# Add and gelu of two flat arrays on one core: rows of 63.5, 64 and 0.5 KB in three blocks instead of rows of 128 KB

## The chip, the core and the metric

The kernel runs on one core of a Trainium2 chip. The core has a tensor engine (PE, not used here), a vector engine (DVE, VectorE), a scalar engine with activation functions (ACT, ScalarE), a general engine (POOL, GpSimd) and a queue engine (SP, SyncE) that here issues the transfers between DRAM (HBM) and the on-chip memory SBUF. The transfers are carried out by 16 DMA engines. SBUF has 128 partitions; a tile here is 128 rows, one a partition. The metric is the device time of one execution in microseconds.

## The reference

Two float32 arrays of 1024 x 4096 are added, and the tanh form of gelu is taken of the sum, element by element:

```python
z = x + y
return (0.5 * z * (1 + np.tanh(np.sqrt(2 / np.pi) * (z + 0.044715 * z ** 3)))).astype(np.float32)
```

Each array is 16.78 MB. Two are read and one is written: 50.33 MB. As every element stands by itself, an array may be cut into rows in any way, as long as x, y and the output are cut alike.

## The kernel before

Each array is seen as 128 rows of 32768 elements (TOT, 128 KB), one a partition (line 88). SBUF holds one tile z of 128 x 32768 for x, the sum and the result, and one tile y of 128 x 16384 (HALF), half a row, that y's two halves use one after the other. A small tile `one` serves to load the activation table early.

There are six transfers, two loads of x, two of y and two stores, each of 128 rows of 64 KB (lines 91 to 93: the halves of the rows). All are issued on SP's queue in a fixed order: y's first half, x's first half, x's second half, y's second half, the first store, the second store. `begin_early` moves the first two ahead of the barrier at the program's start. The second y load overwrites the y tile, so it waits for the adds of the first half. Each store waits for the gelus of its half. `wait_late` lets the program's end clean up while the last store runs, and makes only ACT wait for that store's landing.

The compute goes by 20 chunks of columns (line 94: two of 1024, seven of 2048, 512, 1536, six of 2048, 1024, 512, 512). Chunks 0 to 8 are the first half and 9 to 19 the second. An add (z + y into z) runs on DVE, for chunks 7, 8 and 12 on POOL. For some chunks (`copies`) ACT first copies z to PSUM, a second on-chip memory, and DVE's add reads one operand from there. ACT then takes the gelu of each chunk in place (`on_scalar` is ACT's order). `held` makes POOL's first add wait for DVE's add of chunk 1. A chunk waits for the loads that its columns lie in, by the overlap of column ranges (`over`, `needs`).

The order on each engine is written out by hand: four lists (`sp`, `pool`, `acts`, `dve`), issued as soon as what `needs` names has been issued. The waits on the chip follow from the tiles.

Of the kernel before, what the change touches and what calls it, by code (L numbers as in the profile page):

```python
# [66 lines left out]
def kernel(  # L67
# [12 lines left out]
    nc = tc.nc  # L80
    P = nc.NUM_PARTITIONS
# [3 lines left out]
    N, D = x.shape  # L85
    assert N % P == 0
    TOT = N // P * D
    xv, yv, ov = (a.rearrange("(p n) d -> p (n d)", p=P) for a in (x, y, out))

    HALF = TOT // 2  # L90
    xloads = [HALF, HALF]
    yloads = [16384, 16384]
    stores = [16384, 16384]
    chunks = [1024, 1024] + [2048] * 7 + [512, 1536] + [2048] * 6 + [1024, 512, 512]
    copies = {2: 0, 3: 2048, 4: 0, 5: 2048, 6: 0, 9: 0, 10: 512, 11: 2048}
    on_vector = [0, 1, 2, 3, 4, 5, 6, 9, 10, 11, 13, 14, 15, 16, 17, 18, 19]
# [4 lines left out]
    def ranges(sizes):  # L101
        ends = [sum(sizes[: i + 1]) for i in range(len(sizes))]
        assert ends[-1] == TOT
        return [(e - f, e) for e, f in zip(ends, sizes)]

    xr, yr, sr, cr = (ranges(r) for r in (xloads, yloads, stores, chunks))
# [4 lines left out]
    def over(rs, lo, hi):  # L111
        return [i for i, (a, b) in enumerate(rs) if a < hi and b > lo]
# [6 lines left out]
    zt = pool_sb.tile([P, TOT], fp32, tag="z", name="z")  # L119
    yt = pool_y.tile([P, HALF], fp32, tag="y", name="y")  # L120
# [6 lines left out]

    def load_x(i):
        a, b = xr[i]
        nc.sync.dma_start(out=zt[:, a:b], in_=xv[:, a:b])  # L130

    def load_y(i):
        a, b = yr[i]
        o = a % HALF
        nc.sync.dma_start(out=yt[:, o : o + b - a], in_=yv[:, a:b])  # L135

    def store(i):
        a, b = sr[i]
        nc.sync.dma_start(out=ov[:, a:b], in_=zt[:, a:b])

    def copy(c):
        a, b = cr[c]
# [21 lines left out]
    def earlier_user(c):  # L164
        lo, hi = copies[c], copies[c] + chunks[c]
        before = [k for k in copies if k < c and copies[k] < hi and copies[k] + chunks[k] > lo]
        return [(add, k) for k in before]

    sp = [(load_y, i) for i in over(yr, 0, HALF)] + [(load_x, 0), (load_x, 1)]
    sp += [(load_y, i) for i in over(yr, HALF, TOT)]  # L170
    sp += [(store, i) for i in range(len(stores))]
    pool = [(add, c) for c in on_gpsimd]
    dve = [(add, c) for c in on_vector]
# [3 lines left out]
        load_x: lambda i: [],  # L177
        load_y: lambda i: [(add, c) for c in over(cr, yr[i][0] - HALF, yr[i][1] - HALF)],
        copy: lambda c: [(load_x, i) for i in over(xr, *cr[c])] + earlier_user(c),
        add: lambda c: [(load_x, i) for i in over(xr, *cr[c])]  # L180
        + [(load_y, i) for i in over(yr, *cr[c])]
        + [(copy, k) for k in copies if k == c]
        + [(add, k) for h, k in held.items() if h == c],
# [55 lines left out]
```

## Time and profile before

| | |
|---|---|
| time, median of 3 runs | 120.08 us (119.96 to 120.28) |
| span of the profiled execution | 118.68 us (118.7 on the page) |
| around the span, to the median | 1.40 us |
| moved | 50.33 MB in 864 packets, 424 GB/s over the span |
| busy: DMA engines, ACT, DVE, POOL | 98.5%, 37%, 25%, 12% |
| first y load | issued at 0.00, first packet at 1.01 us |
| x's first half has landed | 41.3 us |
| second y load | issued at 54.86, landed at 80.0 us |
| stores | issued at 77.16 and 97.64 us |

The profiled execution has no device time of its own beside its span, so the median stands for it. A page gives the span, each engine's busy time, the DMA packets with their sizes, and the chain of work that ended last. A packet is one row's piece that one DMA engine moves; the trace has the begin, duration and size of each. A transfer here also has one packet of 4 bytes on each DMA engine, which tells the semaphore of its end. L130, L135 and L139 are the lines that issue x's loads, y's loads and the stores; L150 is the add, L162 the gelu and L143 the copy.

### The profile page before, as it was taken

Reading aid. Unit: us, or ns where it says so; the run is one execution under the profiler, and the core shown is the slowest. Engines: PE = TensorE matmul, PEld = TensorE weight load, DVE = VectorE, ACT = ScalarE, POOL = GpSimd, SP = SyncE. Lnnn points to the kernel's source line nnn. Section 1 sums busy time; section 2 is a strip of 40 time slices with the busy share of each in tenths; the row PEclk is TensorE's granted clock in tenths of the full one; section 3 lists DMA queues with packets and bytes.
Section 4 is the critical chain, followed back from the end, with each engine's and each line's share of the span. In section 5 each row is a group of like instructions: output and inputs, shape, how many; then the busy total and the mean of one; then the engine's idle time right before and its main releaser. Section 6 shows DMA issues by size and latency. Waiting matters only on the chain.

```text
span 118.7 us, 112 instructions
## 1 busy us (share of the span) xinstructions
DVE 29.1 (25%) x18; ACT 44.1 (37%) x30; POOL 13.8 (12%) x7
## 2 busy tenths in 40 slices
DVE  0000000000000099994000000009999920000000
ACT  5000000000000096792059999903799980000000
POOL 0000000000000029980000000009500000000000
DMA  9889988998899888998899888998899888988891
GB/s 353 353 375 641 398 353 353 596 464 353 353 420 618 376 353 353 618 442 353 353 508 552 353 353 375 641 398 353 353 552 508 353 353 353 707 353 353 353 641 66
DMA packets 864, 50.33 MB, mean 424 GB/s; under 512 B 96, under 2 KB 96, under 8 KB 96
## 3 DMA queue, kind: packets, MB, share of 16 engines
q1 hardware_dynamic: 864, 50.33, 98.5%
HBM read 33.55 MB, written 16.78 MB: 424 GB/s over the span
## 4 chain that ended last, share of the span: by engine, by line
DMA 56%; DVE 14%; ACT 10%; DVEq 1%; ACTq 0%; SPq 0%; issue 0%
DMA z<-in_x_dram 34%; DMA y<-in_y_dram 21%; DVE z L150 14%; ACT z L162 10%; DVEq L206 1%; ACTq L206 0%; SPq L135 0%; DVEq L150 0%
## 5 line engine op out<-in xcount | busy, mean ns | idle before, releaser
L162 ACT ACTIVATE z<-z 128x2048 f32<-128x2048 f32 (+3 forms) x20 | 29.7, 1555 | 5.5 <-DVE z L150 5.5
L143 ACT COPY ps<-z 128x2048 f32<-128x2048 f32 (+2 forms) x8 | 13.0, 1654 | 46.8 <-DMA z<-in_x_dram 45.1
L150 DVE TENSOR_TENSOR z<-z,y 128x2048 f32<-128x2048 f32 (+2 forms) x9 | 13.6, 1574 | 40.0 <-DMA z<-in_x_dram 40.0
L150 DVE TENSOR_TENSOR z<-ps,y 128x2048 f32<-128x2048 f32 (+2 forms) x8 | 15.6, 2016 | 25.4 <-DMA y<-in_y_dram 25.4
L150 POOL TENSOR_TENSOR z<-z,y 128x2048 f32<-128x2048 f32 x3 | 13.5, 4529 | 70.7 <-DVE z L150 43.4
L191 ACT ACT_TABLE_LOAD x1 | 1.3, 1283 | 1.3 <-PEq L223 1.3
L190 DVE MEMSET one<- 128x1 f32 x1 | 0.1, 59 | 1.3 <-PEq L223 1.3
L191 ACT ACTIVATE one<-one 128x1 f32<-128x1 f32 x1 | 0.2, 203 | 0.0
L223 POOL MEMSET const-float32-0.0<- 128x1 f32 x1 | 0.1, 99 | 0.2 <-issue 0.2
L223 POOL MEMSET const-bfloat16-1.0<- 128x1 bf16 x1 | 0.1, 102 | 0.0
L223 POOL MEMSET const-uint8-127<- 128x1 uint8 x1 | 0.1, 102 | 0.0
L223 POOL MEMSET const-float32-1.0<- 128x1 f32 x1 | 0.1, 99 | 0.0
## 6 DMA issues: line engine op xcount, KB each, us to landing
y<-in_y_dram SPq DMA_DIRECT2D x2, 23.6
z<-in_x_dram SPq DMA_DIRECT2D x2, 50.1
out_dram<-z SPq DMA_DIRECT2D x2, 21.6
```

What stands on the lines that cost most here:

```text
L143: nc.scalar.copy(out=in_psum(c), in_=zt[:, a:b])
L150: ins = eng.tensor_add(out=zt[:, a:b], in0=first, in1=yt[:, o : o + b - a])
L162: nc.scalar.activation(out=zt[:, a:b], in_=zt[:, a:b], func=act.Gelu_apprx_tanh)
L190: nc.vector.memset(one[:, :1], 0.0)
L191: nc.scalar.activation(out=one[:, :1], in_=one[:, :1], func=act.Gelu_apprx_tanh)
L206: tc.compile()
L223: nc = _bacc.Bacc("TRN2", target_bir_lowering=False, num_devices=1)
```

## The change

The flat arrays are cut in another way. Of the columns 0 to 32767 of the on-chip tile, columns 0 to 16255 (63.5 KB a row) come from the first 128 x 63.5 KB of the array, columns 16384 to 32767 (64 KB a row) from the next 128 x 64 KB, and columns 16256 to 16383 (512 bytes a row) from the last 128 x 512 bytes. Each block is contiguous in DRAM, and its rows follow one another in it.

So there are nine transfers instead of six: for x, y and the output, one of 128 rows of 63.5 KB, one of 128 rows of 512 bytes and one of 128 rows of 64 KB. The order on SP's queue is y 63.5, x 63.5, y 0.5, x 0.5, x 64, y 64, and the stores 63.5, 0.5 and 64. The two that go ahead of the barrier are y 63.5 and x 63.5. The chunks and the engines' orders stay. Chunk 8 (columns 14336 to 16383) now straddles two transfers, so its add waits for four loads' semaphores and its gelu stands before two stores. The second y load of 64 KB rows overwrites what two loads have filled. The store of 64 KB rows uses a semaphore that the first load had used, so that POOL's clearing of semaphores at the end falls into two pieces.

```diff
-    xv, yv, ov = (a.rearrange("(p n) d -> p (n d)", p=P) for a in (x, y, out))
+    blocks = [(0, 16256), (16384, TOT), (16256, 16384)]
+
+    def rows(array, lo, hi):
+        flat, at = array.rearrange("n d -> (n d)"), 0
+        for f, e in blocks:
+            if f <= lo and hi <= e:
+                own = flat[P * at : P * (at + e - f)].rearrange("(p c) -> p c", p=P)
+                return own[:, lo - f : hi - f]
+            at += e - f
+        raise AssertionError((lo, hi))
 
     HALF = TOT // 2
-    xloads = [HALF, HALF]
-    yloads = [16384, 16384]
-    stores = [16384, 16384]
+    xloads = [16256, 128, HALF]
+    yloads = [16256, 128, HALF]
+    stores = [16256, 128, HALF]
...
-        nc.sync.dma_start(out=zt[:, a:b], in_=xv[:, a:b])
+        nc.sync.dma_start(out=zt[:, a:b], in_=rows(x, a, b))
...
-        nc.sync.dma_start(out=yt[:, o : o + b - a], in_=yv[:, a:b])
+        nc.sync.dma_start(out=yt[:, o : o + b - a], in_=rows(y, a, b))
...
-        nc.sync.dma_start(out=ov[:, a:b], in_=zt[:, a:b])
+        nc.sync.dma_start(out=rows(out, a, b), in_=zt[:, a:b])
...
-    sp = [(load_y, i) for i in over(yr, 0, HALF)] + [(load_x, 0), (load_x, 1)]
-    sp += [(load_y, i) for i in over(yr, HALF, TOT)]
+    sp = [(load_y, 0), (load_x, 0), (load_y, 1), (load_x, 1), (load_x, 2), (load_y, 2)]
     sp += [(store, i) for i in range(len(stores))]
```

## The prediction

> **What bounds the kernel now.** I read the page's totals first, then the chain that ended last, then the DMA engines stretch by stretch, and last the very first and last packets. The page:
>
> ```profile
> span 118.7 us, 112 instructions
> ...
> DVE 29.1 (25%) x18; ACT 44.1 (37%) x30; POOL 13.8 (12%) x7
> ...
> DMA packets 864, 50.33 MB, mean 424 GB/s; under 512 B 96, under 2 KB 96, under 8 KB 96
> ...
> q1 hardware_dynamic: 864, 50.33, 98.5%
> ```
>
> No engine that computes is busy for more than 37%, while the 16 DMA engines are busy for 98.5%. The packet counts say how the data travels: six transfers, each with 128 packets of 64 KB (one row of a partition) and 16 of 4 bytes (one per DMA engine, the semaphore): 6 x 144 = 864. So a DMA engine carries 48 large packets, eight per transfer, one after another. The chain of waits, four of its pieces:
>
> ```profile
> 0.43 40.89 DMA z<-in_x_dram
> ...
> 54.86 25.15 DMA y<-in_y_dram
> ...
> 84.72 11.86 ACT z L162 x7
> ...
> 97.09 0.52 ACT z L162
> ```
>
> It changes to compute twice, but only because a store's issue waits for a gelu. The stretches of the span show whether the transfers ever waited for that compute (columns: stretch, its length, busy time of DVE, ACT and POOL, clock, DMA share, GB/s):
>
> ```profile
> 5.00:41.00 36.00, 0.00 (x0) 0.00 (x0) 0.00 (x0) 1.00 1.00 435
> 42.00:59.00 17.00, 12.78 (x7) 10.56 (x7) 9.02 (x2) 1.00 1.00 432
> 100.00:117.00 17.00, 0.00 (x0) 0.00 (x0) 0.00 (x0) 1.00 1.00 432
> ```
>
> Loads alone, loads beside all three engines, and stores alone run at the same 432 to 435 GB/s with share 1.00. The bound is the rate of the DMA engines, in every stage. What is not at that rate is the start. The DMA view of four windows (a packet is booked in the window in which it begins, so a share may pass 100%); 1.0 to 1.5 us, 1.5 to 4.0, 115 to 117, and 117 to 119:
>
> ```profile
> DMA packets 14, 0.92 MB, mean 1835 GB/s; under 512 B 0, under 2 KB 0, under 8 KB 0
> q1 hardware_dynamic: 14, 0.92, 562.3%
> ...
> DMA packets 2, 0.13 MB, mean 52 GB/s; under 512 B 0, under 2 KB 0, under 8 KB 0
> q1 hardware_dynamic: 2, 0.13, 12.3%
> ...
> q1 hardware_dynamic: 16, 1.05, 120.9%
> ...
> q1 hardware_dynamic: 16, 0.00, 0.5%
> ```
>
> Share times window times 16 over the packets is the time of one: 5.623 x 0.5 x 16 / 14 = 3.21 us for the 14 packets that begin together, 0.123 x 2.5 x 16 / 2 = 2.46 us for the two that begin later, 1.209 x 2 x 16 / 16 = 2.418 us in the last stores, and 10 ns for a 4-byte packet (9 ns in its record). By the packet records the 14 begin from 1.01 to 1.45 us and the two at 1.84 and 2.15. Their ends spread from 4.06 to 4.78, and this spread stays: each transfer ends 0.5 to 0.7 us apart on the 16 engines, and the engine whose first packet ended at 4.78 is the last of the first transfer (4.78 + 7 x 2.418 = 21.70; its last semaphore packet is at 21.69). What that packet loses, the span loses.
>
> **The change, part by part.** The durations are of the profiled execution: span 118.68 us, and 1.40 us around it make the median of 120.08.
>
> *Row pitch.* Rows of one transfer lay 128 KB apart in DRAM; in the first transfer of y and x and the first store they now lie 63.5 KB apart, in the second ones 64 KB. In the steady state this has nothing to win: 2.418 us per 64 KB is the same for reads and writes. Only the first packets can gain. They are not simply longer by a latency, or the two late ones would be too; a crowd of 14 engines that begin together, each four rows (512 KB) beyond the last, is what is slow, and I read it as a clash of addresses in DRAM. At 63.5 KB the engines stand 254 KB apart, no power of two. No row shows this pitch, so bounds. If nothing changes, 0. If all packets took 2.418 us and began as now, the last ends at 2.15 + 2.42 = 4.57: gain 0.21. If all begin with the first, 1.01 + 2.42 = 3.43: gain 1.35. In between, the two late starts come into the crowd's window (last at 1.45): 3.87, gain 0.91. A loss is not excluded either: a worse clash would at the nearest row add the worst first packet's excess once more, 3.36 - 2.42 = 0.94. I take 0.91, because in the trace the late ones ran at full speed once others were ahead, so I take their lateness for the same queue.
>
> The Trainium skill's "DMA: Bandwidth & Descriptors", Latency and other measured facts, gives rates by row pitch: 207 GB/s at 512 KiB against 214 for a padded pitch, and half of that from 4 MiB. By it 128 KB costs next to nothing, which agrees with 435 GB/s after 5 us and speaks against any gain; the sum without the gain is the second case below.
>
> *Small packets.* Three transfers of 128 rows of 512 bytes are added (y, x and the store), eight packets and one semaphore packet per DMA engine each. In return 24 of the 48 large packets shrink from 64 to 63.5 KB. A 4-byte packet takes 9 ns; if 9 of the 2418 ns are that fixed part, 64 KB moves in 2409, 512 bytes in 18.8. The shrinking saves 24 x 18.8 = 0.45 us, the small ones cost 24 x (18.8 + 9) = 0.67, the semaphores 3 x 9 = 0.03: net +0.25 us. It lies wholly on the path, since the DMA engines are the path. Lower end: no fixed part, +0.03. Upper end: the eight small packets expose a start each time, the worst first packet's excess of 0.94 us per transfer, 2.8 in all. I take +0.25, because at the five borders between transfers that the trace has, a DMA engine goes from 64 KB over the 4-byte packet to the next 64 KB without a break (at the first, one engine's 4-byte packet runs from 21.608 to 21.617 us and a 64 KB packet begins at 21.614): the queue is fetched ahead.
>
> The same page of the Trainium skill, Rules for kernel authors, says of transfers under 64 KB that one pays mostly overhead, and its Measured table has 0.95 us for 64 KB, the size of each added transfer. Three at that time instead of 0.15 of bandwidth would be +2.4 us; no row of this trace shows such a transfer, and this speaks against the change.
>
> *Issues and waits.* SP gains three issues of some 0.35 to 0.6 us. y's and x's small loads stand ahead of the third load, all issued by about 3 us; the third load's packets are first due at 40.3, so 37 us cover it. The second y load waits for the adds of chunks 0 to 8, now over two loads' worth of buffer; it is issued at 54.86 and its packets are due from 59.66, 0.85 us after an issue at the store's pace: spare 3.9. The small store waits for nothing new and stands behind the large one (77.16), due when that ends at 98.4. The last store is the tight one: issued at 97.64, and the first three engines, done at 98.38 to 98.42, begin it only at 98.49 to 98.52. Issue to packet is thus 0.85 us, and the cover is gone for the earliest engines by 0.1 us; the latest, which sets the end, still has 98.99 - 98.49 = 0.5. Its gelus follow the second y load's landing by 17.6 us, and between that landing and the last store lie now more packets, not fewer, so the cover grows. POOL's chunk 8 (columns 14336 to 16384) straddles the border and waits for the small loads too: these land well under 2 us after x's first load, while POOL works on chunk 7 until 48.4. POOL at the end clears semaphores in two pieces instead of one, under 20 us of the last store.
>
> *Sum.* 118.68 - 0.91 + 0.25 = 118.02 us of span, and 1.40 around it: 119.4 us, 0.55% less. Differences under 0.3% (0.36 us) I count as none; it is about what a measurement can tell here.
>
> **The rivals.** *The small transfers are dear.* Place: the three borders where eight rows of 512 bytes stand between long rows. Price: each exposes part of the start that the first packets show, up to 0.94 us, so at half of it +1.4 and in full +2.8: with no start gain 121.5 and 122.9, with it 120.6 and 122.0. For it: nothing in the trace reads less than 64 KB, so that reads are fetched far enough ahead is not shown; the packets that cross the border without a break are writes of 4 bytes. Against it: the unbroken borders. It decides from 0.12 us per transfer beyond bandwidth on if the start gains nothing, from 0.42 if it gains 0.91.
>
> *The start is no clash.* The 0.7 us come from cold memory or the ramp of 16 engines whatever their addresses; then only +0.25 stays: 120.3, within 0.3%. For it: the page's rates and the full speed of the same pitch from the second packet on. Against it: the two fast late packets.
>
> *The clash moves or the late starts stay.* The gain is only 0.21, or the 64 KB rows (engines 256 KB apart) clash at the third load, which used to find the engines spread over 0.7 us. Then -0.21 + 0.25 or -0.91 + 0.91 + 0.25: 120.1 to 120.3, no difference.
>
> **How the numbers follow.** Start gain with cheap small packets (119.4): 0.43, faster. No clash (120.3): 0.13; gain small or moved (120.1): 0.11; together 0.24 the same. Dear small transfers (120.5 to 122.9): 0.33, slower. The range begins with the whole start gain and free small packets, 120.08 - 1.35 + 0.03 = 118.8, and reaches into the third case to half price without gain, 121.5, which leaves out about 1.5 in 10. The likeliest case alone is 118.8 to 119.7.
>
> **What would show it.** Right: first packets near 2.4 us and their last end before 4.0; 512-byte packets near 28 ns; the DMA engines at share 1.00 across the new borders. Wrong: first packets of 3 us again; idle time or 512-byte packets of 50 ns and more around 20, 40 and 98 us; a third load whose first packets are longer than 2.42; a last store that begins late on the last engine.

## The result, and the profile after

| | before | changed |
|---|---|---|
| median | 120.07 us (20 runs, 119.94 to 120.38) | 120.36 us (20 runs, 120.05 to 120.80) |
| ratio | | 1.0023, 95% interval 1.0015 to 1.0031 |
| span of the profiled execution | 118.7 us | 119.1 us |

The change costs 0.2%, 0.29 us by the medians. The forecast was 119.4 us. The profiled execution took 120.61 us itself, so it lies above its own median; sizes are taken from the medians, and the profile shows where things stand.

The page of the changed kernel:

```profile
span 119.1 us, 120 instructions
...
DVE 29.1 (24%) x18; ACT 44.1 (37%) x30; POOL 13.8 (12%) x7
...
DMA packets 1296, 50.33 MB, mean 423 GB/s; under 512 B 144, under 2 KB 528, under 8 KB 528
...
q1 hardware_dynamic: 1296, 50.33, 98.3%
```

The compute is the same to the tenth. The packets went from 864 to 1296: 384 of 512 bytes and 48 more of 4 bytes. The chain of waits, and the stretches (length, busy time of DVE, ACT and POOL, clock, DMA share, GB/s):

```profile
0.42 40.82 DMA z<-in_x_dram
...
54.77 25.59 DMA y<-in_y_dram
...
85.07 11.86 ACT z L171 x7
...
97.44 0.52 ACT z L171
```

```profile
5.00:39.00 34.00, 0.00 (x0) 0.00 (x0) 0.00 (x0) 1.00 0.99 428
42.00:59.00 17.00, 12.70 (x7) 10.48 (x7) 9.02 (x2) 1.00 1.00 432
100.00:117.00 17.00, 0.00 (x0) 0.00 (x0) 0.00 (x0) 1.00 1.00 432
```

The same bound, at the same rate. The first stretch is 0.99 because a packet is booked where it begins, and the stretch here ends between two packets. What was to be shorter is the first packets; the DMA view from 1.0 to 1.5 us:

```profile
DMA packets 14, 0.91 MB, mean 1821 GB/s; under 512 B 0, under 2 KB 0, under 8 KB 0
...
q1 hardware_dynamic: 14, 0.91, 534.7%
```

That is 5.347 x 0.5 x 16 / 14 = 3.06 us a packet; at the later rate 63.5 KB take 2.40. Before it was 3.21 against 2.42. By the packet records the mean over all 16 engines is 3.08 us (3.12 before). The ends lie from 3.87 to 4.56, and the first packet of one engine, which took 3.90, ends at 4.99, where the latest ended at 4.78 before. So the start gain of 0.91 us did not come. The 512-byte packets took 27 ns, all 384 of them.

### The profile page after: what moved, and what is told of

Same layout as the page of the kernel before. It is cut to its first block, busy times and chain, and to the rows that moved or that the text cites. A ratio compares the mean times of both kernels' runs of the same rounds, so it can differ in the third digit from the quotient of the medians.

```text
span 119.1 us, 120 instructions
## 1 busy us (share of the span) xinstructions
DVE 29.1 (24%) x18; ACT 44.1 (37%) x30; POOL 13.8 (12%) x7
## 2 busy tenths in 40 slices
DMA packets 1296, 50.33 MB, mean 423 GB/s; under 512 B 144, under 2 KB 528, under 8 KB 528
## 3 DMA queue, kind: packets, MB, share of 16 engines
q1 hardware_dynamic: 1296, 50.33, 98.3%
## 4 chain that ended last, share of the span: by engine, by line
DMA 56%; DVE 14%; ACT 10%; DVEq 1%; ACTq 0%; SPq 0%; issue 0%
DMA z<-in_x_dram 34%; DMA y<-in_y_dram 21%; DVE z L159 14%; ACT z L171 10%; DVEq L214 1%; ACTq L214 0%; SPq L144 0%; DVEq L159 0%
```

## The experiments

Two readings stood against each other at first: that the small packets are all that the change costs and the row pitch does nothing (theory A), and that the short pitch costs and the small packets are free (theory B). Against both stood the forecast's own, that the first packets clash by their addresses. All ratios are to runs of the kernel before on the same chip.

### The pitch alone, and the nine transfers alone

Two blocks of 64 KB rows, no small transfers:

```diff
+    blocks = [(0, HALF), (HALF, TOT)]
-    xloads = [16256, 128, HALF]
+    xloads = [HALF, HALF]
```

(and so for y and the stores; the issues of the small transfers are left out.)

> Two blocks of 128 rows of 64 KB (row pitch 64 KB), six transfers, no 512-byte packets. Theory A (small packets: what the change costs is 24 packets of 512 bytes on each DMA engine, 27 ns each, and the start does not depend on the pitch): as the kernel before, ratio 0.999 to 1.001, 14 or so first packets at 3.0 to 3.4 us. Theory B (the short pitch costs: a worse latest engine at the start, small packets free): ratio 1.002 to 1.003. The clash of the forecast, if only 63.5 KB had missed to cure it: first packets worse or as before.

Measured: 120.17 us, ratio 1.0005 (0.9992 to 1.0018). First packets 3.16 us in the mean, none under 2.8.

The nine transfers, at the old pitch:

```diff
-    blocks = [(0, 16256), (16384, TOT), (16256, 16384)]
+    blocks = [(0, TOT)]
```

> The nine transfers of the change (rows of 63.5, 0.5 and 64 KB) with the row pitch of 128 KB of the kernel before. Theory A: as the changed kernel, ratio 1.0015 to 1.003, 512-byte packets of 27 ns. Theory B: ratio 0.999 to 1.001.

Measured: 120.12 us, 1.0002 (0.9986 to 1.0017). Neither part alone makes the 0.2%, to the accuracy of these runs, so both readings missed: each had put 0.15% or more on one of these two kernels.

Only y's first load at 63.5 KB pitch, all else as before:

```diff
+        src = yv[:, a:b]
+        if i == 0:
+            src = bass.AP(tensor=src.tensor, offset=0, ap=[[16256, P], [1, b - a]])
-        nc.sync.dma_start(out=yt[:, o : o + b - a], in_=yv[:, a:b])
+        nc.sync.dma_start(out=yt[:, o : o + b - a], in_=src)
```

> The kernel before, with y's first load alone reading 128 rows of 64 KB at a pitch of 63.5 KB (so the rows overlap and the first half of y is other data than the reference's). Six transfers. Theory A: ratio 0.999 to 1.001, first packets' mean still 3.0 to 3.2 us. Theory B: ratio 1.002 to 1.003 with a wider spread of the first packets' ends. The clash of the forecast: ratio 0.992 to 0.995, first packets near 2.42 us.

Measured: 120.23 us, 1.0003 (0.999 to 1.0016), first packets 3.11 us in the mean. The forecast's clash is out: the very pitch that was to cure it, alone, changes nothing that can be measured.

### Small loads first

```diff
-    sp = [(load_y, 0), (load_x, 0), (load_y, 1), (load_x, 1), (load_x, 2), (load_y, 2)]
+    sp = [(load_y, 1), (load_y, 0), (load_x, 1), (load_x, 0), (load_x, 2), (load_y, 2)]
```

> The changed kernel with the 512-byte loads of y and x issued ahead of the 63.5 KB ones. If the 0.7 us that the first packets take more is a first access whatever the size, the small packets take it, the first long packets run at 2.40 us, and the ratio stays 1.002 to 1.003. If it belongs to 16 engines beginning long rows at once, the first 65024-byte packets still take about 3.0 us, and the small packets' cost stands beside it: 1.002 to 1.004.

Measured: 120.81 us, 1.0057 (1.0038 to 1.0075), dearer than either reading said. The DMA view of 1.0 to 1.45 us and of 1.45 to 4.0:

```profile
DMA packets 144, 0.07 MB, mean 146 GB/s; under 512 B 16, under 2 KB 144, under 8 KB 144
...
q1 hardware_dynamic: 144, 0.07, 50.8%
...
DMA packets 16, 1.04 MB, mean 408 GB/s; under 512 B 0, under 2 KB 0, under 8 KB 0
...
q1 hardware_dynamic: 16, 1.04, 120.3%
```

The 512-byte packets begin at 1.01 us, as the first packets of the kernel before do; most take 25 or 27 ns and are through by 1.4; the first long packets begin from 1.5 us on, as SP's second issue comes 0.4 us after the first, and take 1.203 x 2.55 x 16 / 16 = 3.07 us all the same. So the small transfer took none of the start away. The 0.5 us by which the long rows begin later were not in my expectation; with the 0.3 us of the change itself they come to 0.8, near the 0.7 measured.

### The hardest clash: all rows from one address

Against the kernel with y's first load at 63.5 KB:

```diff
-            src = bass.AP(tensor=src.tensor, offset=0, ap=[[16256, P], [1, b - a]])
+            src = bass.AP(tensor=src.tensor, offset=0, ap=[[0, P], [1, b - a]])
```

> The kernel before, with y's first load reading the same 64 KB of DRAM for all 128 rows (the first half of y is other data than the reference's): the hardest clash of addresses there can be. If the 0.7 us of the first packets are a clash of addresses: first packets well over 3.3 us and the whole first load slower than 2.42 us a packet, ratio over 1.005. If addresses don't matter to it: first packets 3.0 to 3.3 us, ratio 0.999 to 1.001.

Measured: 120.30 us, 1.0011 (0.9997 to 1.0024). DMA view from 1.0 to 1.5 us:

```profile
DMA packets 14, 0.92 MB, mean 1835 GB/s; under 512 B 0, under 2 KB 0, under 8 KB 0
...
q1 hardware_dynamic: 14, 0.92, 467.7%
```

Packets of 4.677 x 0.5 x 16 / 14 = 2.67 us, shorter than ever; but by the records they begin later, from 1.28 to 1.60 instead of from 1.01, and end from 3.91 to 4.40, near the 4.06 to 4.78 of the kernel before. This is the lesson of the two late packets that misled me. In the kernel before they begin at 1.84 and 2.15 us and end at 4.34 and 4.57, within the ends of the other 14: a later begin and a shorter length came without an earlier end. It is no rule for every packet, as in the trace at pitch 0 those that begin later are the longer ones, and why that load begins later is not shown.

My expectation of 3.0 to 3.3 us missed. The ratio is just above the 0.999 to 1.001 that I had named if addresses don't matter, and far below the 1.005 named for a clash. That one address for all rows is the hardest clash is not shown either, as a repeated row may also be easy to read; the run counts beside those at 63.5 and 64 KB, where the excess stayed too.

### Sixty-four small packets in place of eight

The long rows of the first transfers are cut to 60 KB, and 4 KB a partition go as eight rows of 512 bytes, laid out in DRAM so that they stay apart:

```diff
+    blocks = [(0, 15360), (16384, TOT), (15360, 16384)]
+                if e - f == 1024:
+                    return flat[P * at : P * (at + 1024)].rearrange("(j p c) -> p j c", p=P, j=8)
-    xloads = [16256, 128, HALF]
+    xloads = [15360, 1024, HALF]
```

(and so for y and the stores.)

> Eight times the small packets: the long rows of the first transfers are 60 KB, and the three small transfers have 8 rows of 512 bytes a partition (the last block is laid out piece by piece, so that they don't join). By the steps between packets each engine pays 192 x 24 ns + 18 ns - 24 x 151 ns = +1.0 us: ratio 1.008 to 1.009, packets of 27 ns. If what small packets cost is fetching ahead that runs dry, more than 8 in a row cost more than 27 ns each: ratio 1.012 and up. If they are free: 1.000 to 1.002.

Measured: 121.43 us, 1.0105 (1.0087 to 1.0122), between the two sizes named. The DMA view of 38.8 to 41.0 us, within the two small loads:

```profile
DMA packets 1507, 0.76 MB, mean 347 GB/s; under 512 B 16, under 2 KB 1507, under 8 KB 1507
...
q1 hardware_dynamic: 1507, 0.76, 114.8%
```

1.148 x 2.2 x 16 / 1507 = 26.8 ns a packet, and no dearer with 64 in a row than with eight: the DMA engines move 512-byte rows at 347 GB/s instead of 432. An eighth of the 1.35 us is 0.17 us for the changed kernel's three small transfers. The packet records give a little less: from the end of the latest first packet to the end of the last packet this kernel takes 114.67 us and the kernel before 113.54, and an eighth of that difference is 0.14 us.

### What is left for the pitch

The parts were measured again beside the whole on two more chips, and on a third without it, with one new form: nine transfers in two blocks of 64 KB pitch, the 512-byte rows being the ends of the first block's rows.

```diff
-    blocks = [(0, 16256), (16384, TOT), (16256, 16384)]
+    blocks = [(0, TOT // 2), (TOT // 2, TOT)]
```

The changed kernel and nine transfers at 128 KB, on the first of these chips:

> The changed kernel once more, beside its parts on one chip. Theory A (small packets alone; each engine 24 x 24 ns + 3 x 6 ns - 24 x 19 ns = +0.14 us by the steps between packets of its trace): ratio 1.0012, and like the nine transfers at a pitch of 128 KB. Theory C (small packets +0.14 and, at a row pitch of 63.5 KB, one first packet of 3.9 us that makes the latest engine 0.2 us later): ratio 1.002 to 1.003, and over the nine transfers at 128 KB by 0.001 to 0.002.

> The nine transfers at a row pitch of 128 KB again, for the comparison with the changed kernel on one chip. Theory A: as the changed kernel, both 1.001 to 1.0015. Theory C: 1.001 to 1.0015, the changed kernel above it by 0.001 to 0.002.

On the second chip, these two, nine transfers at 64 KB, and y's first load alone at 63.5 KB:

> The changed kernel, to settle what of its cost is the pitch. Small packets alone (from the eightfold run, 1.30 / 8 = 0.16 us): ratio 1.0013, no more than the nine transfers at the other pitches. If the pitch of 63.5 KB adds a late engine: the latest first packet ends at 4.9 to 5.0 us, 0.3 us or more behind the second latest, and the median lies 0.1 to 0.2 us over the nine transfers at 64 and 128 KB.

> Nine transfers at a pitch of 128 KB: ratio 1.0005 to 1.0015 by either; the first packets' ends within 0.2 us of each other at the late end.

> Nine transfers (rows of 63.5, 0.5 and 64 KB), but in two blocks with a pitch of 64 KB, the 512-byte rows being the ends of the first block's rows. Small packets alone: 1.0005 to 1.0015. If any short pitch costs, as the changed kernel. If only 63.5 KB does: 0.1 to 0.2 us under the changed kernel.

> The kernel before with y's first load alone at 63.5 KB pitch, again (the first half of y is other data than the reference's). If 63.5 KB adds a late engine: latest first packet's end at 4.9 to 5.0 us, 0.3 us or more behind the second latest, ratio 1.001 to 1.002. If that was chance: ends as in the kernel before (4.7 to 4.8, close to the second latest) and ratio 1.000.

On the third chip, nine transfers at 64 and at 128 KB:

> Nine transfers in two blocks of 64 KB pitch, again. If the short pitch costs 0.15 to 0.2 us: ratio 1.0015 to 1.0025 and over the 128 KB pitch by 0.0012 to 0.0017. If that was chance: both 1.0005 to 1.0015, and no more than 0.0005 apart.

> Nine transfers at a pitch of 128 KB, again: ratio 1.0003 to 1.0013 by either.

Median less the median of the kernel before on the same chip, in us, and the ratios:

| kernel | median's difference | ratios with intervals |
|---|---|---|
| changed | 0.29, 0.25, 0.21 | 1.0023 (1.0015 to 1.0031), 1.0016 (1.0002 to 1.0030), 1.0012 (0.9998 to 1.0026) |
| nine, 128 KB | 0.01, 0.12, 0.02, 0.11 | 1.0002, 1.0007, 1.0012, 1.0014, each reaching below 1 |
| nine, 64 KB | 0.25, 0.23 | 1.0020 (1.0007 to 1.0034), 1.0022 (1.0014 to 1.0031) |
| y's first load at 63.5 KB | 0.12, 0.08 | 1.0003, 1.0005, each reaching below 1 |

The nine transfers at 128 KB stand at 0.07 us in the mean, at or under what the small packets alone should cost. With a short pitch beside them it is 0.21 to 0.29, for 64 KB as for 63.5. So by the medians 0.1 to 0.2 us goes with the shorter pitch. By the ratios of kernels measured side by side it is less, 0.0000 to 0.0009 where I had expected 0.001 to 0.002, and the intervals overlap; two of the 128 KB kernels have one run each of 121.2 or 121.3 us. Compared run by run, a run of nine transfers with a short pitch lies above one at 128 KB in 66, 72 and 78% of the pairs on the three chips, where 50% would be no difference. So a difference of about 0.1 us stands, near the limit of what these runs tell.

The packet records give the packets' part free of the start's luck. From the end of the latest first packet to the end of the last packet, the kernel before takes 113.54 us, the 64 KB kernel without small transfers 113.53, and the first trace with y's first load at 63.5 KB 113.52. Four traces of nine transfers at 128 KB have 113.67 to 113.69, so against the kernel before the small packets cost 0.13 to 0.15 there. Three traces of the changed kernel have 113.65 to 113.75, two of nine transfers at 64 KB 113.66 and 113.76.

Two traces without small packets are as long as those, though: the second with y's first load at 63.5 KB has 113.72 and the one at pitch 0 has 113.69. In both, in the two changed kernels at 113.75 and in the 64 KB one at 113.76, the engine that ends last has a single packet that is 0.10 to 0.22 us longer than the usual 2.418. The windows 77.5 to 77.6 us of the changed kernel and 77.2 to 77.4 of y's first load at 63.5 KB hold that one packet each:

```profile
q1 hardware_dynamic: 1, 0.07, 157.8%
...
q1 hardware_dynamic: 1, 0.07, 82.3%
```

That is 1.578 x 0.1 x 16 = 2.52 us and 0.823 x 0.2 x 16 = 2.63. Less this one excess, the three with small packets all have 113.65, and the two without them 113.50 and 113.56. So in the traces the small packets cost the same at each pitch to a few hundredths of a microsecond, and no pitch makes the steady packets longer. Four of the five long packets begin 0.06 to 0.10 us behind the begin of the first store's issue; no run tests whether that is the cause.

Where the pitch's part sits was only half found. In all five traces in which y's first load has 63.5 KB pitch and goes first, one engine is late: its first packet ends at 4.88 to 4.99 us, 0.3 to 0.7 behind the second latest. At other pitches the latest ends at 4.40 to 4.86, at most 0.22 behind the second latest but for one trace of nine transfers at 128 KB, where it is 0.37 and I had expected under 0.2. But y's first load alone at that pitch costs only 0.08 to 0.12 by the medians, and nine transfers at 64 KB have the changed kernel's time without such an engine in the first of their two traces (4.66). Those five profiled executions also took 0.09 to 0.26 us more than the median of their kernel, so the late engine need not be in the median run. What the short pitch costs beside small transfers, and why it costs nothing clear without them, stays open.

### What the start is

With the pitch out of it, the excess of the first packets had to be either a fixed time or a lower rate. The kernel before, with y's first load in two:

```diff
-    yloads = [16384, 16384]
+    yloads = [4096, 12288, 16384]
```

The two issues ahead of the barrier are then both y's, and x's first follows at 1.25 us, long before its packets are due.

> The kernel before, with y's first load split into rows of 16 KB and of 48 KB (pitch 128 KB as before, seven transfers). A 16 KB packet takes 0.61 us by the later packets' rate. If the excess is a fixed time at the head of the first long transfer: the first 16 KB packets take about 1.3 us, the rest of them 0.61, ratio 1.000 to 1.002. If the engines run at three quarters of their rate for the first 3 us, whatever the packets: first packets 0.8 us, and the following three or so also 0.8. If only packets of many KB begun together are slow: 16 KB packets at 0.61 us and the first 48 KB ones 0.7 us longer than 1.81.

Measured: 120.00 us, 0.9989 (0.9978 to 1.0000). DMA view of 1.0 to 1.9 us, then of 1.9 to 2.7. Each holds 16 packets, in the main the first and the second of the 16 engines, though a few second packets begin before the last of the first ones:

```profile
DMA packets 16, 0.26 MB, mean 291 GB/s; under 512 B 0, under 2 KB 0, under 8 KB 0
...
q1 hardware_dynamic: 16, 0.26, 122.9%
...
DMA packets 16, 0.26 MB, mean 328 GB/s; under 512 B 0, under 2 KB 0, under 8 KB 0
...
q1 hardware_dynamic: 16, 0.26, 83.3%
```

In the mean the first packets take 1.229 x 0.9 = 1.11 us, the second 0.833 x 0.8 = 0.67, and the later ones 0.61. With rows of 4 KB (`yloads = [1024, 15360, 16384]`):

> As the 16 KB run, with rows of 4 KB first (0.16 us a packet, eight of them 1.3 us). Fixed head: first packet 0.8 us or so, the others 0.16. Lower rate: all eight about 0.21 us and the first 60 KB ones 0.2 to 0.4 us longer than 2.27. Long packets alone: all eight 0.16 us, the first 60 KB ones 2.9 to 3.2.

Measured: 120.08 us, 0.9989 (0.9979 to 1.0000); windows 1.0 to 1.6 and 1.6 to 2.7:

```profile
DMA packets 16, 0.07 MB, mean 109 GB/s; under 512 B 0, under 2 KB 0, under 8 KB 16
...
q1 hardware_dynamic: 16, 0.07, 95.7%
...
DMA packets 101, 0.41 MB, mean 376 GB/s; under 512 B 0, under 2 KB 0, under 8 KB 101
...
q1 hardware_dynamic: 101, 0.41, 94.9%
```

The first take 0.957 x 0.6 = 0.57 us, the others 0.949 x 1.1 x 16 / 101 = 0.165. By these windows the excess is 0.41 us on a 4 KB packet, 0.50 on 16 KB, 0.70 on 64 KB: far from proportional. As the windows mix first and second packets, it is safer to sum the excess over all 128 packets of the short rows: 0.45 us for each engine at 4 KB, 0.56 at 16 KB. Of these packets 22 and 20 are more than a tenth longer than the usual one, little more than the one for each engine. So it is nearly all a head on each engine's first long packet, and no lower rate. Why it is larger for 64 KB, and why 512-byte rows show none and leave it to the long rows behind them, no run here tells.

Both came out a hair faster, so the 16 KB form was run again, with one of 8 KB beside it:

> The kernel before with y's first load in rows of 16 and 48 KB, again. If the latest engine at the start sets the end and short first rows bring it nearer to the others: ratio 0.998 to 0.9995, first transfer's engines 0.35 to 0.5 us apart. If it was chance: 0.9995 to 1.0005.

> As the 16 KB form, with rows of 8 and 56 KB. First packets about 0.3 + 0.5 = 0.8 us, the others 0.31; ratio as that of 16 KB, 0.998 to 0.9995, if a short first row is what helps.

(`yloads = [2048, 14336, 16384]` for 8 KB.) Measured: 120.01 us, 0.9993 (0.998 to 1.0007), and 120.06 us, 0.9996 (0.9978 to 1.0014). The first 16 packets take 1.10 and 0.68 us in the mean, the latter less than the 0.8 expected, and the summed excess is 0.53 and 0.45 us for each engine. The engines do end the first load's short rows closer together, 0.23 us apart at 16 KB (0.41 in the first run of it) and 0.31 at 8 KB, against 0.71 for the first load of the kernel before. Still, no gain is shown, and no version here surely beats the kernel before.

## Why the prediction was wrong

*The bound* was read rightly: DMA engines at 432 GB/s in every stretch, before and after, so that the change could only act through packets and the start.

*Row pitch* is the step that failed, and the whole of the sign with it. It put 0.91 us of gain on the start, because two first packets that began late ran at full speed, which I took for a clash in DRAM among those that began together. The excess is there at pitches of 63.5, 64 and 128 KB alike, and reading one address from all engines left the ends near where they were. Rows of 4 to 16 KB show instead a head of 0.45 to 0.56 us, about once per engine. So a first packet that begins with the others would not have taken 2.42 us at any of these pitches, which every gain above 0 in the prediction had assumed. The two fast late packets were no sign of a clash, as they ended in the midst of the others. The profile had the material for a better reading: the second packets stood at the same pitch, half of them beginning within 20 ns of the one before, and ran at full rate, which I counted as a point for the rival and gave 0.13. The rates by pitch in the Trainium skill ("DMA: Bandwidth & Descriptors", Latency and other measured facts) speak against a gain at 128 KB; the trace agrees, with 432 GB/s before and after. What the head comes from stays open.

*Small packets* were sized well one by one, 28 ns forecast and 27 measured. Their sum of +0.25 us was too high, against 0.17 by the time of the eightfold run and 0.13 to 0.15 by the records, because a packet begins about 3 ns before the record of the one ahead ends. What counts is the step from one begin to the next: 24 ns for 512 bytes, 6 for 4 bytes, and 19 less for 63.5 KB than for 64. So the fixed part is nearer 6 ns than 9, and the sum is 24 x 24 + 3 x 6 - 24 x 19 = 138 ns. That the packets go on without a break over the borders, which rested on five borders with a 4-byte packet, held for 64 small packets in a row. The rival of dear small transfers, at 0.33, is out with that. The overhead that the Trainium skill ("DMA: Bandwidth & Descriptors", Rules for kernel authors) gives for transfers under 64 KB is not seen here at 64 KB, in a queue that always has the next transfer in it: such a transfer is 8 x 27 ns = 0.22 us on each engine. The 0.95 us in the Measured table of the same page of the Trainium skill is for transfers that GpSimd issues; these are issued by SP, so the prediction's +2.4 us did not follow from it.

*Issues and waits* were costed at nothing. The latest engine did not wait for the last store, as forecast. Most others did: the last store's first packets are at 98.82 us, and by the packet records 14 engines were done with the small store between 98.19 and 98.80; they then stood idle for 0.02 to 0.78 us, where I had argued that the cover grows. It shrank for them, because the second y load landed later, at 80.36 instead of 80.01 us, with its one late engine, and the gelus behind it wait for all engines. It did not set the end: the late engine finished its small store only at 99.42.

*The result* lies in the second case, no clash and only the packets' cost, 120.3 us forecast there and 120.36 measured; it had a chance of 0.13. The whole range 118.8 to 121.5 held it. That it comes so near is in part luck: its 0.25 us was some 0.1 too much for the packets, and it had nothing for the 0.1 us or so that goes with the pitch.

## What to carry to other kernels

Where transfers ran back to back here, the time was in the main the end of the latest first packet, plus packets times their step; both can be read from packet records, and so can a single long packet that adds 0.1 or 0.2 us. A change of row pitch won nothing in a stretch that already ran at its constant step. At the start of a queue compare packet ends and not lengths, and try a suspected clash with one cheap pointer before believing it: one load alone at another pitch. Some 512-byte rows within a full queue are cheap (5 ns each beyond their bytes here), but putting a small transfer first pushed all else back by its issue, 0.4 to 0.5 us.

## What the runs showed that I had not expected

With 64 small packets per engine and transfer, the issue itself stood still. The timeline of SP's queue in that kernel (start, length, engine, line, operation):

```profile
1.25 0.38 SPq L149 DMA_DIRECT2D y<-in_y_dram  x1
1.69 37.37 SPq L144 DMA_DIRECT2D z<-in_x_dram  x2
52.55 0.34 SPq L149 DMA_DIRECT2D y<-in_y_dram  x1
```

The two issues that begin at 1.69 us, x's small load and the third long one, lasted 29.8 and 7.5 us by their records, against 0.3 to 0.5 elsewhere: they stood still while 16 long packets and 64 small ones per engine were queued ahead of the first of them. They ended at 39.06 us, and the third load's first packets began at 41.05, so it was not late. Whether the standstill cost something else is open: at 31.1 to 31.8 us, as the first of the two issues ended, each of the 16 engines has a 60 KB packet that is 0.06 to 0.07 us longer than its others. More small rows ahead of a long load could make the issue the bound; no run shows it.
